# Queries, keys and probabilities turned by DRAM and block transposes, with a pair's steps set wider apart and a second GLU block ahead of the first pair

## The chip, the cores and the metric

The kernel runs on one core of a Trainium2 chip. The time is that of the whole execution in microseconds (us), as the device measures it. Before the change three runs took 1937.97, 1940.64 and 1940.51 us; their median is 1940.51 us. A core has five engines that work side by side, each with its own queue of instructions in a fixed order: PE (matrix multiplication), DVE (elementwise work and block transposes), ACT (activation functions and copies), POOL (here it issues DMAs) and SP (it issues the loads of the weights). An instruction that waits for something holds up everything behind it on its engine.

## The reference

Two layers over 256 positions and 2048 channels, in float32. Each layer normalises its input, multiplies by one wide input matrix, and splits the product into two branches:

```python
h = rmsnorm(x, norm_g)
proj = h @ w_in        # c_a, c_glu, c_gate, q_down, kv_down, k_pe, m_gate, g_conv, g_mla
y_conv = conv_branch(...) @ w_proj_conv   # GLU, causal depthwise conv of width 31, layernorm, silu, gate
y_mla = mla_branch(...) @ w_proj_mla      # q = rmsnorm(q_down) @ w_uq, k and v = rmsnorm(kv_down) @ w_ukv,
                                          # per-head norm, rope, block-causal softmax over 16 heads, gate
y = sigmoid(g_conv) * y_conv + sigmoid(g_mla) * y_mla
return x + y @ w_out
```

A head has 128 channels without position, 64 with rope (the rope key is shared by all heads) and 128 value channels. Positions are in chunks of 64; a query sees the keys of its own and of earlier chunks.

## The kernel before

**Products.** Every product has the activations as stationary operand and streams the weights, in blocks of up to 512 columns. To keep float32 accuracy each weight and each activation is split into a high and a low part, and `product` adds three matmuls: high by high, high by low and low by high (L222 to L224). Weights come in pieces of four 128-row tiles by SP's queue (`load`, L167) into three buffers; `split` makes the high part on ACT (L179) and the low part on DVE (L180) for two tiles at a time, up to two splits ahead of the matmuls, with three buffers of each part. One split feeds twelve matmuls; this is the unit of time of the program, and I call it a slot. A 512-column matmul follows the one before it by 0.227 us, so a slot is 2.73 us.

**Order of the blocks of a layer.** Three blocks of the down projection, GLU block 0, then for each of eight pairs of heads: the queries of the pair (`uq`, 2 slots), its keys and values (`ukv`, 2 slots) and, but for the last, the next GLU block (8 slots). After the pairs come four blocks each of `mgate`, `gmla`, `pmla`, `cgate`, `gconv`, `pconv` and `wout`.

**Work beside the products.** After each slot `background` takes one step from the queue `attn` (the attention of the pairs) and as many from `fill` (the taps of the convolution, two DVE instructions each at L657, and later the layernorm and the gate of branch A) as a budget allows: 0.65 units a slot while pairs run, 0.7 units a tap; from `mgate` on the rest of the fill is spread over the `20 * 8 - 4` slots before `pconv`. A planner then writes each engine's order: it goes by the program's order as priority and by its own estimate of when an instruction's data is there, and it puts the splits 100 instructions sooner (`SPLIT_SOONER`).

**A pair's steps.** `uq_evac` and `ukv_evac` copy the products out of PSUM and sum squares on ACT. Then `attention` appends eight steps, one for each of the next slots: `stats` (the two norms, key scaling and rope, on DVE), `turn_rope` twice, `turn_nope` twice, `scores`, `turn_p`, `values`. The three turning steps transpose 128x128 tiles on PE into PSUM (L537, L524, L599 to L603): 4 for rope, 8 for nope, 6 for the probabilities, and ACT and DVE split what stands in PSUM into high and low parts.

**The other way of turning**, already in use for the GLU and the gates: `park` writes a 128-row tile to DRAM with four DMAs of 32 rows each, so that the 32x32 blocks change places; `fetch` reads it back with one DMA; a DVE instruction transposes each 32x32 block (L257). All these DMAs are issued by POOL (L238, L246), and the fetch waits there until the parks have landed. `turn` puts the DVE step six splits later.

The functions around the change, with the line numbers of the profile:

Of the kernel before, what the change touches and what calls it, by code (L numbers as in the profile page):

```python
# [59 lines left out]
TURNED_AFTER = 6  # L60
SUMS_AFTER = 1
# [19 lines left out]

def blocks_of_layer():

    s = {"win": [], "wuq": [], "wukv": [], "wpc": [], "wpm": [], "wo": []}
    for _, n in DOWN_BLOCKS:
        s["win"].append(n)
    s["win"] += [512] * 24
    s["wuq"] = [2 * QK] * NPAIR
    s["wukv"] = [2 * (NOPE + VH)] * NPAIR
    for w in ("wpc", "wpm", "wo"):  # L90
        s[w] = [512] * 4
    return s
# [3 lines left out]
def trunk(ctx: ExitStack, tc: tile.TileContext, xT, x, g_in, pos, win, wuq, wukv, wpc, wpm, wo, cst, rows, invf, out):  # L96
# [43 lines left out]
    for l in range(DEPTH):  # L140
        order = [("down", i, "win") for i in range(len(DOWN_BLOCKS))] + [("glu", 0, "win")]
        for b in range(NPAIR):
            order += [("uq", b, "wuq"), ("ukv", b, "wukv")]
            if b + 1 < 8:
                order.append(("glu", b + 1, "win"))
        for kind, s in (
            ("mgate", "win"), ("gmla", "win"), ("pmla", "wpm"),
            ("cgate", "win"), ("gconv", "win"), ("pconv", "wpc"), ("wout", "wo"),
        ):
            order += [(kind, i, s) for i in range(4)]  # L150
        plans.append([(k, i, plan(l, s)) for k, i, s in order])

    loaded, done = {}, {}
# [16 lines left out]
    def split(i):  # L170
# [10 lines left out]
        done[i] = hi, lo  # L181
        while deferred and deferred[0][0] <= i:
            with tc.issue_after(ins.ins):
                deferred.popleft()[1]()
# [5 lines left out]
    budget = {"fill": 0.0, "rate": 0.0, "slots": 0}  # L190

    def background():
# [51 lines left out]
    def fetch(d, n):  # L244
        z = wide_p.tile([P, 4, n // P, 32], F32, tag="w", name="turned")
        nc.gpsimd.dma_start(z.rearrange("p i c s -> p (i c s)"), d.rearrange("j s i e -> (j s) (i e)"))  # L246
        return z

    def turn(src, n, use, dst=None):
# [3 lines left out]
        z = fetch(park(src, n, turn_d), n)  # L253
# [119 lines left out]
    for l in range(DEPTH):  # L373
# [85 lines left out]
        def pair_of(b, pairs=pairs, v_split=v_split):  # L459
            if b not in pairs:  # L460
                pairs[b] = dict(
                    q=work2.tile([P, T, 2, QK], F32, tag="q", name="q"),
                    k=work2.tile([P, T, 2, NOPE], F32, tag="k", name="k"),
                    r=work2.tile([P, 2, T, 2, ROPE], F32, tag="r", name="r"),
# [6 lines left out]
        def uq_evac(b, t, ps, pair_of=pair_of):  # L471
            p = pair_of(b)
            nc.scalar.copy(p["q"][:, t].rearrange("p h d -> p (h d)"), ps)
            for h in range(2):
                junk = work.tile([P, 512], F32, tag="junk", name="junk")
                nc.scalar.activation(
                    junk[:, :QK], ps[:, h * QK : (h + 1) * QK], AF.Square, accum_out=p["ss"][:, 0, t, h : h + 1]
                )

        def ukv_evac(b, t, ps, pair_of=pair_of):  # L480
            p = pair_of(b)
            v = ps.rearrange("p (h a d) -> p h a d", h=2, a=2)
            nc.scalar.copy(p["vh"][:, t], v[:, :, 1, :])
            nc.vector.tensor_sub(p["vl"][:, t], v[:, :, 1, :], p["vh"][:, t].bitcast(F32))
            nc.scalar.copy(p["k"][:, t], v[:, :, 0, :])
            for h in range(2):
                junk = work.tile([P, 512], F32, tag="junk", name="junk")
                nc.scalar.activation(junk[:, :NOPE], v[:, h, 0, :], AF.Square, accum_out=p["ss"][:, 1, t, h : h + 1])

        def attention(b, pair_of=pair_of, ss_d=ss_d, kpe=kpe, ccq=ccq, ssq_t=ssq_t, gqk=gqk, nope_t=nope_t, rope_t=rope_t, rope_k=rope_k, rope_l=rope_l, o_sb=o_sb, pt_h=pt_h, pt_l=pt_l, rinv=rinv):  # L490
# [3 lines left out]
            def stats():  # L494
                ss, q, k = p["ss"], p["q"], p["k"]
# [7 lines left out]
                rk = r[:, 1].unsqueeze(3)  # L503
                nc.vector.tensor_mul(k, k, rk.broadcast_to([P, T, 2, NOPE]))
                nc.vector.tensor_mul(
                    p["r"][:, 1], kpe.unsqueeze(2).broadcast_to([P, T, 2, ROPE]), rk.broadcast_to([P, T, 2, ROPE])
                )
                qr = q[:, :, :, NOPE:]
                qa = work.tile([P, T, 2, ROPE], F32, tag="qa", name="qa")
                qb = work.tile([P, T, 2, ROPE], F32, tag="qb", name="qb")  # L510
                nc.vector.tensor_mul(qa, qr, ccq.unsqueeze(2).broadcast_to([P, T, 2, ROPE]))
                nc.vector.tensor_mul(qb, qr, ssq_t.unsqueeze(2).broadcast_to([P, T, 2, ROPE]))
                qr = p["r"][:, 0]
                nc.vector.tensor_sub(qr[:, :, :, :HALF], qa[:, :, :, :HALF], qb[:, :, :, HALF:])
                nc.vector.tensor_add(qr[:, :, :, HALF:], qb[:, :, :, :HALF], qa[:, :, :, HALF:])
# [3 lines left out]
            def turn_nope(which):  # L519
                src = p["qk"[which]]  # L520
                tp = tp_p.tile([P, 2, SEQ], F32, tag="tp", name="tp_qk")
                for h in range(2):
                    for t in range(T):
                        nc.tensor.transpose(tp[:, h, t * P : (t + 1) * P], src[:, t, h, :NOPE], ident)  # L524
                hi, lo = nope_t[:, 2 * which], nope_t[:, 2 * which + 1]
                if which == 0:
                    nc.scalar.activation(hi, tp, AF.Copy, scale=gqk)
                    nc.vector.scalar_tensor_tensor(lo, tp, gqk, hi.bitcast(F32), op0=ALU.mult, op1=ALU.subtract)
                else:
                    nc.scalar.copy(hi, tp)  # L530
                    nc.vector.tensor_sub(lo, tp, hi.bitcast(F32))

            def turn_rope(which):
                src = p["r"][:, which]
                tp = tp_p.tile([P, SEQ], F32, tag="tp", name="tp_rope")
                for t in range(T):
                    nc.tensor.transpose(tp[:, t * P : (t + 1) * P], src[:, t].rearrange("p h d -> p (h d)"), ident)  # L537
                for h in range(2):
                    own, other = halves[h], halves[1 - h]
                    nc.scalar.copy(rope_t[own, which, h, :], tp[own])  # L540
                    if which == 0:
                        nc.vector.tensor_sub(rope_t[other, 0, h, :], tp[own], rope_t[own, 0, h, :].bitcast(F32))
                    else:
                        nc.scalar.copy(rope_t[other, 1, h, :], tp[own])
                        nc.vector.tensor_sub(rope_l[own, h, :], tp[own], rope_t[own, 1, h, :].bitcast(F32))

            def scores():
# [30 lines left out]
                pr = work.tile([P, 2 * P + 2 * SEQ], F32, tag="pr", name="pr")  # L578
                sums = small.tile([P, T, 2], F32, tag="sums", name="sums")
                at = 0  # L580
                st["pr"] = []
                for t, s, nkeys in ((0, s0, P), (1, s1, SEQ)):
                    for h in range(2):
                        dst = pr[:, at : at + nkeys]
                        nc.scalar.activation(
                            dst, s[:, h, :], AF.Exp,
# [3 lines left out]
                        st["pr"].append(dst)  # L590
                        at += nkeys
# [394 lines left out]
```

## Time and profile before

| | |
|---|---|
| median of the runs | 1940.51 us |
| the profiled execution | 1937.65 us, span 1935.8 us |
| PE busy | 1923.1 us, 99% of the span |
| DVE busy | 1582.1 us, 82% |
| ACT busy | 1101.3 us, 57% |
| POOL busy | 233.1 us, 12% |
| moved by DMA | 399.82 MB, 207 GB/s on the mean |
| granted TensorE clock | 1.0 throughout |

The span is the time from the first to the last instruction; the execution has 1.85 us around it. A row of a group of instructions reads: line, engine, operation, written tile <- read tiles, shape, count | busy time in us, mean length of one in ns | idle time of the engine just before them, and what ended most of it. Instructions of one engine overlap at their ends, so a group's busy time can be less than count times length. A row of waits reads: who <- for whom: us in total, times, longest.

By the order of the evacuations, the first layer has its GLU blocks and pairs from about 80 to 350 us, `mgate`, `gmla` and `pmla` to about 618, `cgate` and `gconv` to about 797, then `pconv` and `wout`; the second layer repeats this some 960 us later.

### The profile page before, as it was taken

What the parts mean: (1) busy time and instruction counts of PE and PEld (TensorE: products, weight loads), DVE (VectorE), ACT (ScalarE), POOL (GpSimd) and SP (SyncE); (2) the same over time, 40 slices, a digit from 0 to 9 for tenths busy, and PEclk for the clock granted to TensorE, in tenths of its full rate; (3) what the DMA queues carried; (4) which work ended last, traced back from release to release, by engine and by line L of the source; (5) the groups of instructions that cost most, each with busy time, mean ns of one, the idle gap of its engine ahead of it and who ended that gap; (6) DMA issues with size and microseconds to landing.
All of it is one profiled execution on the core that took longest, in us unless ns stands there. A gap on an engine that the chain in (4) does not pass through costs nothing.

```text
span 1935.8 us, 25532 instructions
## 1 busy us (share of the span) xinstructions
PE 1923.1 (99%) x9069; PEld 1623.8 (84%) x9069; DVE 1582.1 (82%) x2820; ACT 1101.3 (57%) x1750; POOL 233.1 (12%) x444
## 2 busy tenths in 40 slices
PE   9999999999999999999999999999999999999999
PEld 8888888888888887888898888888888888878887
DVE  7789998999999987466657899889999999864654
ACT  6667767664444457444556676776654435564443
POOL 0111111121000120021301121121210002101200
PEclk9999999999999999999999999999999999999999
DMA  7655555566555665566865554555665556655674
GB/s 290 220 178 182 185 177 183 192 212 228 191 191 193 216 243 190 201 240 231 272 237 196 180 190 176 179 187 200 218 218 196 196 191 212 239 191 206 241 254 142
DMA packets 72592, 399.82 MB, mean 207 GB/s; under 512 B 13056, under 2 KB 13072, under 8 KB 33552
## 3 DMA queue, kind: packets, MB, share of 16 engines
q1 hardware_dynamic: 55728, 361.44, 52.6%
q0 software_dynamic: 16736, 36.74, 6.0%
q8 instruction: 71, 1.16, 0.2%
q14 instruction: 57, 0.47, 0.1%
HBM read 376.64 MB, written 21.50 MB: 206 GB/s over the span
## 4 chain that ended last, share of the span: by engine, by line
PE 96%; DVE 1%; ACT 1%; issue 1%; DMA 0%; SPq 0%; DVEq 0%; ACTq 0%
PE acc L223 31%; PE acc L222 31%; PE acc L224 31%; PE o_ps L615 1%; PE s L569 1%; PE tp_qk L524 1%; ACT hi L179 1%; DVE v_t L700 0%; PE tp_rope L537 0%; DMA raw<-in_win 0%; ACT ycT L808 0%; DVE turned L798 0%; DVE v_t L802 0%; PE s L555 0%; DVE lo L180 0%
## 5 line engine op out<-in xcount | busy, mean ns | idle before, releaser
L179 ACT CAST hi<-raw 128x1024 fp32r<-128x1024 f32 (+2 forms) x688 | 703.5, 1024 | 716.8 <-PE acc L224 536.3
L180 DVE TENSOR_TENSOR lo<-raw,hi 128x1024 fp32r<-128x1024 f32 (+2 forms) x688 | 816.9, 1189 | 264.2 <-ACT hi L179 261.9
L657 DVE SCALAR_TENSOR_TENSOR v_t<-u_t,cst,v_t 128x256 f32<-128x256 f32 x960 | 414.9, 481 | 1.1
L223 PE MATMUL acc<-lo,h_hi 128*128 128x512 f32 (+2 forms) x864 | 334.3, 387 | 1.4 <-DVE lo L180 1.4
L223 PE MATMUL acc<-lo,hT 128*128 128x512 f32 (+2 forms) x864 | 333.3, 386 | 1.4 <-DVE lo L180 1.3
L224 PE MATMUL acc<-hi,h_lo 128*128 128x512 f32 (+2 forms) x864 | 331.7, 384 | 0.0
L224 PE MATMUL acc<-hi,hT 128*128 128x512 f32 (+2 forms) x864 | 331.0, 383 | 0.0
L222 PE MATMUL acc<-hi,h_hi 128*128 128x512 f32 (+2 forms) x864 | 302.5, 385 | 3.5 <-ACT hi L179 3.5
L222 PE MATMUL acc<-hi,hT 128*128 128x512 f32 (+2 forms) x864 | 301.8, 384 | 0.7 <-ACT hi L179 0.7
L238 POOL DMA_DIRECT2D turn_d<-gate x176 | 95.5, 550 | 803.7 <-ACT gate L792 459.4
L222 PEld LDWEIGHTS acc<-hi,h_hi 128*128 128x128 f32 x864 | 162.0, 189 | 34.0 <-ACT hi L179 4.7
L223 PEld LDWEIGHTS acc<-lo,h_hi 128*128 128x128 f32 x864 | 163.0, 189 | 32.5 <-DVE lo L180 3.8
L223 PEld LDWEIGHTS acc<-lo,hT 128*128 128x128 f32 x864 | 162.3, 188 | 32.0 <-DVE lo L180 3.3
L224 PEld LDWEIGHTS acc<-hi,h_lo 128*128 128x128 f32 x864 | 163.0, 189 | 28.9
L222 PEld LDWEIGHTS acc<-hi,hT 128*128 128x128 f32 x864 | 161.4, 188 | 30.6 <-ACT hi L179 1.1
L224 PEld LDWEIGHTS acc<-hi,hT 128*128 128x128 f32 x864 | 162.3, 188 | 28.8
L238 POOL DMA_DIRECT2D turn_d<-su x128 | 69.6, 550 | 484.2 <-DVE su L637 474.1
L223 PE MATMUL acc<-lo,yT 128*128 128x512 f32 x256 | 100.0, 390 | 0.0
L224 PE MATMUL acc<-hi,yT 128*128 128x512 f32 x256 | 99.6, 389 | 0.0
L223 PE MATMUL acc<-lo,ycT 128*128 128x512 f32 x256 | 99.6, 389 | 0.0
L224 PE MATMUL acc<-hi,oT 128*128 128x512 f32 x256 | 99.6, 389 | 0.0
L224 PE MATMUL acc<-hi,ycT 128*128 128x512 f32 x256 | 99.6, 389 | 0.0
(206 smaller groups left out, 2494.0 us busy)
## 6 DMA issues: line engine op xcount, KB each, us to landing
raw<-in_win SPq DMA_DIRECT2D x192, 1024.0 KB, 4.8
raw<-in_wpm SPq DMA_DIRECT2D x32, 1024.0 KB, 4.7
raw<-in_wpc SPq DMA_DIRECT2D x32, 1024.0 KB, 4.8
raw<-in_wo SPq DMA_DIRECT2D x32, 1024.0 KB, 4.9
raw<-in_wukv SPq DMA_DIRECT2D x16, 1024.0 KB, 4.7
turned<-turn_d POOLq DMA_DIRECT2D x50, 256.0 KB, 4.3
raw<-in_wuq SPq DMA_DIRECT2D x16, 768.0 KB, 4.3
raw<-in_win SPq DMA_DIRECT2D x15, 768.0 KB, 6.8
```

Of the source, the lines that this page charges most:

```text
L179: nc.scalar.copy(hi, r)
L180: ins = nc.vector.tensor_sub(lo, r, hi.bitcast(F32))
L222: nc.tensor.matmul(pts[t][:, :n], sh, hi[:, kk, :], start=first, stop=False)
L223: nc.tensor.matmul(pts[t][:, :n], sh, lo[:, kk, :], start=False, stop=False)
L224: nc.tensor.matmul(pts[t][:, :n], sl, hi[:, kk, :], start=False, stop=last)
L238: nc.gpsimd.dma_start(d[:, :, i, :].rearrange("j s e -> s j e"), src[32 * i : 32 * i + 32, :].rearrange("s (j e) -> s j e", j=4),)
L524: nc.tensor.transpose(tp[:, h, t * P : (t + 1) * P], src[:, t, h, :NOPE], ident)
L569: nc.tensor.matmul(s1[:, h, :], qa, ka, start=n == 0, stop=n == len(terms) - 1)
L615: nc.tensor.matmul(o_ps[:, h, kt * P :], v[j][:, kt, h, :], pt[i][:, h, queries], start=n == 0, stop=n == len(todo) - 1,)
L657: nc.vector.scalar_tensor_tensor(dst, src, w, dst, op0=ALU.mult, op1=ALU.add)
```

## The change

Queries, keys and probabilities are no longer transposed on PE. The columns of `w_uq` and `w_ukv` are put in another order ahead of the run, so that a pair's scaled keys, queries and both rope parts stand in one tile `qk` of 768 columns for each half of the positions, cut into 32-column blocks. `stats` writes them there and then parks and fetches each half in place; nine slots later `blockwise` transposes the blocks on DVE in place, and `split_rope` and `split_nope` make high and low parts from SBUF. The query gain is now applied in place on ACT ahead of the split. `scores` writes the probabilities of a pair into one tile of 768 columns and parks and fetches it; six slots later `split_p` transposes its blocks and splits it in two instructions.

The steps have slots of their own (`at_slot`): statistics in the first slot after the pair's keys, 60 instructions sooner in the planner's order; blocks and rope at 9, nope at 10 and 11, scores at 14, probabilities at 20, values at 22. Before, the eight steps took slots 1 to 8. The block transposes are put behind the newest low split on DVE (`issue_after`).

GLU blocks 0 and 1 both come ahead of the first pair, block `b + 2` follows pair `b`, and `cgate` block 0 stands between pairs 6 and 7. The fill's rate beside GLU blocks falls from 0.65 to 0.55 units a slot, and the slots over which the rest is spread from `20 * 8 - 4` to `19 * 8 - 4`. The layernorm's work tiles move to the new tile's buffers.

```diff
+QK_AFTER = 9
+P_AFTER = 6
...
+def order_of_layer():
+
+    order = [("down", i, "win") for i in range(len(DOWN_BLOCKS))] + [("glu", 0, "win"), ("glu", 1, "win")]
+    for b in range(NPAIR):
+        order += [("uq", b, "wuq"), ("ukv", b, "wukv")]
+        if b + 2 < 8:
+            order.append(("glu", b + 2, "win"))
+        elif b + 1 < NPAIR:
+            order.append(("cgate", 0, "win"))
...
+    def at_slot(ahead, f):
+        steps.append((clock[0] + ahead, f))
+
     def background():
+        clock[0] += 1
         if attn:
             attn.popleft()()
+        due = [f for slot, f in steps if slot <= clock[0]]
+        steps[:] = [e for e in steps if e[0] > clock[0]]
+        for f in due:
+            f()
...
-    def fetch(d, n):
+    def fetch(d, z):
+        nc.gpsimd.dma_start(z, d.rearrange("j s i e -> (j s) (i e)"))
...
+                qk=work2.tile([P, T, 4, 6, 32], F32, tag="qk", name="qk"),
+                qr=work2.tile([P, T, 2, 2, HALF], F32, tag="qr", name="qr"),
...
+            nc.scalar.copy(p["qk"][:, t, :, 0:2, :], ps[:, : 2 * NOPE].rearrange("p (j h c) -> p j h c", j=4, h=2))
+            nc.scalar.copy(p["qr"][:, t].rearrange("p a h c -> p (a h c)"), ps[:, 2 * NOPE :])
...
+                for t in range(T):
+                    rk = r[:, 1, t, :]
+                    k = qk[:, t, :, 2:4, :]
+                    nc.vector.tensor_mul(k, k, rk.unsqueeze(1).unsqueeze(3).broadcast_to([P, 4, 2, 32]))
...
+                for t in range(T):
+                    rows = qk[:, t].rearrange("p j i c -> p (j i c)")
+                    fetch(park(rows, 768, turn_d), rows)
...
-            def turn_nope(which):
...
+            def blockwise():
+                for t in range(T):
+                    z = p["qk"][:, t].rearrange("p j i c -> p (j i c)")
+                    with tc.issue_after(newest[0]):
+                        nc.vector.transpose(z, z)
+
+            def split_nope(which):
+                z = back[:, :, 2 * which : 2 * which + 2, :].rearrange("p b h s -> p h b s")
+                hi, lo = (nope_t[:, 2 * which + i].rearrange("p h (b s) -> p h b s", s=32) for i in range(2))
                 if which == 0:
+                    nc.scalar.activation(z, z, AF.Copy, scale=gqk)
+                nc.scalar.copy(hi, z)
+                nc.vector.tensor_sub(lo, z, hi.bitcast(F32))
...
-            def turn_p():
...
+                st["pr"] = pr.rearrange("p j h x c -> p (j h x c)")
+                fetch(park(st["pr"], 768, turn_d), st["pr"])
+
+            def split_p():
+                z = st["pr"]
+                with tc.issue_after(newest[0]):
+                    nc.vector.transpose(z, z)
+                z = z.rearrange("p (b i s) -> p i b s", i=6, s=32)
+                hi, lo = (a.rearrange("p h (x b s) -> p (h x) b s", x=3, s=32) for a in (pt_h, pt_l))
+                nc.scalar.copy(hi, z)
+                nc.vector.tensor_sub(lo, z, hi.bitcast(F32))
...
-            attn.append(stats)
-            for turn in (turn_rope, turn_nope):
-                for which in range(2):
-                    attn.append(lambda turn=turn, which=which: turn(which))
-            attn.extend((scores, turn_p, values))
+            def stats_soon():
+                with tc.high_priority(offset=60):
+                    stats()
+
+            at_slot(0, stats_soon)
+            at_slot(QK_AFTER, lambda: (blockwise(), split_rope(0), split_rope(1)))
+            for which in range(2):
+                at_slot(QK_AFTER + 1 + which, lambda which=which: split_nope(which))
+            at_slot(QK_AFTER + 5, scores)
+            at_slot(QK_AFTER + 5 + P_AFTER, split_p)
+            at_slot(QK_AFTER + 7 + P_AFTER, values)
...
-                budget["rate"] = 0.65
+                budget["rate"] = 0.55
...
-                    budget["slots"] = 20 * 8 - 4
+                    budget["slots"] = 19 * 8 - 4
```

More of the change, by code (lines that the diff above doesn't have):

```diff
@@ L140, in trunk @@
     for l in range(DEPTH):
[L141 to L153, printed above, removed]
+        plans.append([(k, i, plan(l, s)) for k, i, s in order_of_layer()])
+    loaded, done, newest = {}, {}, [None]
     deferred = deque()
@@ L533, in turn_rope @@
[L533 to L537, printed above, removed]
+                for t in range(T):
+                    rk = r[:, 1, t, :]
+                    k = qk[:, t, :, 2:4, :]
+                    nc.vector.tensor_mul(k, k, rk.unsqueeze(1).unsqueeze(3).broadcast_to([P, 4, 2, 32]))
+                    nc.vector.tensor_mul(
+                        qk[:, t, :, 5, :].rearrange("p (h a) c -> p h a c", h=2),
+                        kpe[:, t].rearrange("p (a c) -> p a c", a=2).unsqueeze(1).broadcast_to([P, 2, 2, HALF]),
+                        rk.unsqueeze(2).unsqueeze(3).broadcast_to([P, 2, 2, HALF]),
+                    )
@@ L538, in turn_rope, with split_rope @@
+            def split_rope(which):
+                z = back[:, :, 4 + which, :]
+                rt, rl = (a.rearrange("p i h (b s) -> p i h b s", s=32) for a in (rope_t, rope_l.unsqueeze(1)))
                 for h in range(2):
                     own, other = halves[h], halves[1 - h]
[L540 removed]
+                    nc.scalar.copy(rt[own, which, h], z[own])
                     if which == 0:
[L542 removed]
+                        nc.vector.tensor_sub(rt[other, 0, h], z[own], rt[own, 0, h].bitcast(F32))
```

150 lines of the change are left out of this document (71 added, 79 removed).

## Prediction

> **What bounds the kernel now.** I read the page's busy shares and its chain of waits first, then the waits of PE, then the groups of instructions with shapes kept apart, a timeline of PE where probabilities are turned, and a table of stages.
>
> ```profile
> PE 1923.1 (99%) x9069; PEld 1623.8 (84%) x9069; DVE 1582.1 (82%) x2820; ACT 1101.3 (57%) x1750; POOL 233.1 (12%) x444
> PE 96%; DVE 1%; ACT 1%; issue 1%; DMA 0%; SPq 0%; DVEq 0%; ACTq 0%
> PE acc L222 <- ACT hi L179: 4.2, 3, 2.8
> PE acc L223 <- DVE lo L180: 2.7, 4, 0.8
> ```
>
> PE is 99% busy, the chain is 96% PE, and PE waits 6.9 us in all for split weights. So an instruction taken from PE's queue comes off the time, as long as no new wait appears there.
>
> ```profile
> 215.48 0.27 PE L601 MATMUL tp_p<-ident,pr 128*128 128x128 f32 x1
> 215.59 0.27 PE L603 MATMUL tp_p<-ident,pr 128*128 128x128 f32 x1
> 215.70 0.27 PE L601 MATMUL tp_p<-ident,pr 128*128 128x128 f32 x1
> 215.80 0.27 PE L603 MATMUL tp_p<-ident,pr 128*128 128x128 f32 x1
> 215.83 0.48 PE L223 MATMUL acc<-lo,h_hi 128*128 128x512 f32 x1
> 216.15 0.39 PE L224 MATMUL acc<-hi,h_lo 128*128 128x512 f32 x1
> ```
>
> This timeline (start, length) gives the price of a transpose. Its length is 0.27 us, but the next one starts 0.11 us later; four of them and one 512-column matmul (pace 0.227 us elsewhere) take 216.15 - 215.48 = 0.67 us, so one costs (0.67 - 0.227)/4 = 0.11 us.
>
> ```profile
> 160.00:320.00 160.00, 160.00 (x817) 137.28 (x816) 146.40 (x327) 116.51 (x252) 24.86 (x47) 1.00 0.52 179
> 480.00:600.00 120.00, 120.00 (x531) 99.42 (x530) 116.27 (x206) 53.21 (x56) 0.00 (x0) 1.00 0.54 193
> 690.00:760.00 70.00, 67.91 (x294) 54.45 (x293) 61.58 (x93) 48.16 (x65) 8.61 (x16) 1.00 0.61 216
> 760.00:800.00 40.00, 40.00 (x178) 33.15 (x177) 17.58 (x16) 18.31 (x19) 0.00 (x0) 1.00 0.56 202
> ```
>
> Columns: stretch, length, busy PE, PEld, DVE, ACT, POOL, clock, DMA share, GB/s. In the pairs (160 to 320) DVE is at 91.5%; under the taps (480 to 600) it reaches 96.9% with PE still full, the highest load here that costs PE nothing; by 760 to 800 it is at 44%. DVE is the next limit.
>
> **The change, part by part.**
>
> *Transposes leave PE.* A pair has 4 rope, 8 nope and 6 probability transposes: 18, times 16 pairs is 288. At 0.11 us that is 31.7 us, all on the path. Nothing is added to PE.
>
> *DVE work per pair,* by the means of these rows:
>
> ```profile
> L180 DVE TENSOR_TENSOR lo<-raw,hi 128x768 fp32r<-128x768 f32 x64 | 61.1, 956 | 21.5 <-ACT hi L179 21.4
> L257 DVE STREAM_TRANSPOSE turned<-turned 128x512 f32<-128x512 f32 x34 | 24.0, 706 | 3.3 <-DMA turned<-turn_d 3.3
> L257 DVE STREAM_TRANSPOSE u_t<-turned 128x256 f32<-128x256 f32 x32 | 14.1, 440 | 5.5 <-DMA turned<-turn_d 5.5
> L504 DVE TENSOR_TENSOR k<-k,r_p 128x512 f32<-128x512 f32 x16 | 10.9, 684 | 0.0
> ```
>
> Three block transposes of 128x768: from 440 ns (256) and 706 (512) I extend to 0.97 us each, +2.91. The key multiply of 512 (0.684) becomes two of 256 (0.418 each, L511): +0.15. The shared-key multiply of 256 (0.415) becomes two of 128 (0.285, L514): +0.16. The low part of the queries loses its scale (0.746 to 0.685): -0.06. The low parts of probabilities, 0.686 + 0.417, become one of 768 (0.956): -0.15. Sum +3.0 us a pair, 24 us a layer, 48 us in all. Reading 32-element runs costs nothing extra: L750 does so and takes 685 ns, like the plain 512s.
>
> What covers it: DVE is idle 720 - 638 = 82 us between 80 and 800 of the first layer (the seven-stage table of that stretch). PE's time there falls by 8 x 2.0 = 16 us, which leaves 82 - 24 - 16 = 42 us, 94% load; below the 96.9% that cost PE nothing. Within the pairs it is tighter: a period is 36.3 us now (the first query evacuations of pairs 1 and 6 start at 118.84 and 300.25: 181.4/5), and DVE does 91.5%, 33.2, of it. After: 33.2 + 3.0, less 1.4 because the tap rate falls from 0.65 to 0.55 (12 slots x 0.1/0.7 = 1.7 taps, two instructions each at a pace of 0.4), is 34.8 in 34.3. So about 0.5 to 1.5 us of taps a period must slip past the last pair. They can: splits are ordered ahead of taps, and the taps' deadline is the last cgate/gconv stretch with the 44% above. If this cover is gone, PE pays the excess itself (first rival).
>
> *ACT per pair:* the query evacuation of 384 (0.481) becomes 256 (0.370) and 128 (0.28), twice: +0.34; the in-place scale (0.688) is now followed by a copy (0.614, L749): +0.61; probabilities in one copy: -0.12. +0.83 us a pair on an engine 73% busy in this stage (116.51 of 160): to 80%, no cost; ACT's longest queue is the hi copies, which wait for PE. The gate block moved between pairs 6 and 7 may add a table load or two of 1.28 us, covered likewise.
>
> *POOL and its queue:* 15 more DMAs a pair at 0.55 us, 8.3 us in a period of 34.3 on an engine 16% busy: to 40%. Between parks and the fetch POOL stands 1.9 to 5.0 us; now the two parks of queries and keys, the park of probabilities and the two GLU parks share the queue, and the GLU block's fetch can be queued behind a fetch that has not its data. In the gate blocks eight parks go out side by side (4.33 us), so the two query parks need not stand behind the first fetch.
>
> *DMA:* 3 x 0.393 MB out and back is 2.4 MB a pair, 69 GB/s on top of 179; the first 40 us of the kernel move 318 GB/s. No cost; the raw weight loads, landing in 4.8 us, may land some tenths later, ahead of their use by two pieces.
>
> *Latency of a turn, a new wait.* A GLU turn in the trace: first park at 198.54, fetch at 205.28, DVE reads at 209.00: 10.5 us; four parks 2.2, gap 3.5, issue 0.56, landing 3.7. For 768 columns in pairs of turns: 4.4 + 3.5 + 1.1 + about 5 (256 KB lands in 4.3) = 14 us. Ahead of it the statistics (204.92 to 213.9: 9 us). 23 us, against QK_AFTER = 9 slots, that is 8 x 2.73 after the step, plus 2 of scores: 23. Probabilities: scores to last exponential 9.5 us (203.9 to 213.4) and a turn of 12: 21, against 6 slots: 16. So a transpose can come up in DVE's queue as much as 5 us ahead of its data. It is pinned only behind the newest low split, so while DVE stands there the next low split stands too; PE holds up to two splits (5.5 us). Bounds: 0, as the GLU turns cost DVE 5.5 us and PE nothing, to 3 us a pair (5 us less a lead of 2; PE's weight loads stood for a low split 11 times, 1.2 us at most, so its lead is not always the full 5.5). I take 0.15 us a pair, 2 us in all, as the nearest row is the GLU turn itself, built and queued alike; and the written order is no deadline, for o_ps already comes 47 us after the pair's key evacuation (95.9 to 143.3), where eight slots would be 22: the planner puts a step where it expects its data.
>
> Tile for tile, the rows above make a 128x128 transpose 0.11 us on PE and 0.97/6 = 0.16 on DVE, with five DMAs for six of them; only PE's share lies on the path now. The Trainium skill, "VectorE: DVE Perf Modes", Rules for kernel authors, says to transpose 128x128 on TensorE where a PSUM destination will do, which speaks against this change. By that rule, the sum would be 288 x 0.05 = 14 us slower instead of 31.7 faster, were DVE's share on the path as PE's is. The trace agrees with it on the two prices; that DVE's share reaches the path is the first and second rival.
>
> *Second GLU block ahead, gate block later:* the same blocks of PE work in another order; zero. It gives taps work before the first pair. The number of slots after the pairs falls from 156 to 148, 22 us less in which the fill runs; with 42 us of DVE idle left I cost it at zero.
>
> *Sum:* -31.7 + 2 = -29.7. Against the profiled execution, 1937.65 (span 1935.8 and 1.85 around it): 1908. The median shown is 1940.51, 2.9 above; against it 1910.8. I give 1911.
>
> **The rivals.**
> 1. *DVE becomes the bound in the pairs and its taps do not slip.* For: 34.8 us of work in 34.3. At the best load seen, 96.9%, the period is 35.9 instead of 34.3: 1.6 us lost in about 14 periods, 23 us: 1934. Against: the planner already lets pair steps lag by 25 us and more.
> 2. *Late turns stop the low splits (the other side).* DVE stands in front of a transpose whose fetch has not landed, the next low split stands behind it, and PE after the 2 us lead. 3 us a pair is 48 us: 1940.5 - 31.7 + 48 = 1957. It decides from 2.0 us a pair. For: the 5 us computed for probabilities, POOL's five turns in a period, DVE with no idle time to catch up. Against: the GLU turns cost PE nothing.
> 3. *The two nearly cancel:* some periods of each, within 0.2%.
> That the transposes stay on PE is excluded by the diff.
>
> **How the numbers follow.** Forecast 0.54 (its own range 1904 to 1919), first rival 0.12 (of it 0.02 no change), second 0.30, the third 0.02, others 0.02, half of them faster. Faster 0.54 + 0.10 + 0.01 = 0.65; same 0.02 + 0.02 = 0.04; slower 0.30 + 0.01 = 0.31. A change under 0.2% (4 us) can't be told from none here. The range goes from 1903 (the full 31.7 off the lowest run shown, 1938, and most of the 2.1 us a layer that PE stands between 690 and 760, 67.91 of 70, should the new order of the fill remove it) to 1958, the second rival's price; its worse half lies outside.
>
> **What would show it.** Right: no L524/L537/L599-603 group, PE's matmul count lower by 288, PE still 99%, DVE near 85% overall, three 768-wide block transposes a pair at 0.97 us, DVE idle before them under 1 us each, PE waits for low splits under 10 us. First rival: DVE over 97% and PE under 97% between 160 and 340. Second: large idle before the block transposes released by DMA, PE waiting on L180's successor, or key/value evacuations held because the values step of two pairs before is late. Wrong also if the fill ends late and PE stands at the first pconv block.

## The result: slower, 2069.78 us

The changed kernel takes 2069.78 us in the median (2067.96 to 2070.27), against 1940.58 for the kernel before on the same chip: a ratio of 1.0666, 95% interval 1.0648 to 1.0685. The prediction was 1911 us, with 1958 as its upper end; it is wrong by sign and by size, 129 us the other way. The profiled execution has a span of 2068.0 us and a mean granted clock of 0.971.

The page of the kernel after: the row of busy times, and the row of the chain of waits.

```profile
PE 1950.6 (94%) x8781; PEld 1626.1 (79%) x8781; DVE 1624.3 (79%) x2884; ACT 1126.4 (54%) x1786; POOL 365.4 (18%) x684
...
PE 70%; DVE 14%; ACT 7%; DMA 5%; issue 3%; POOL 2%; ACTq 0%; SPq 0%; DVEq 0%; POOLq 0%
```

The 288 transposes are gone (9069 - 8781), but PE stands: 94% busy instead of 99%, and the chain is 70% PE instead of 96%. DVE, the engine I feared, is at 79%, less than before. Where the chain now runs is told by the table of stages of the kernel after, in its first layer (stretch, length, busy PE, PEld, DVE, ACT, POOL, granted clock, DMA share, GB/s):

```profile
200.00:240.00 40.00, 34.88 (x152) 29.20 (x151) 27.00 (x64) 23.78 (x52) 11.99 (x22) 0.87 0.52 165
240.00:280.00 40.00, 29.15 (x122) 24.41 (x121) 30.40 (x71) 22.28 (x55) 8.09 (x16) 0.83 0.44 151
...
400.00:440.00 40.00, 30.91 (x124) 25.44 (x125) 26.86 (x64) 21.00 (x50) 8.19 (x15) 0.75 0.41 138
...
480.00:720.00 240.00, 238.14 (x1066) 196.46 (x1065) 225.43 (x381) 118.75 (x137) 25.22 (x46) 1.00 0.60 214
```

From 480 to 800 us PE is full (from there to 960 us the gaps hold 5 us). Nearly all is lost in the pairs, and there no engine is near its limit: in 240 to 280, PE 73%, DVE 76%, ACT 56%, and the DMA engines 44%, where they had 55% in the same stretch before. So it is latency, a chain of waits, that sets the pace. Taking the starts of consecutive matmuls, gaps of over 0.7 us hold 120 us of standing (beyond a matmul's pace of 0.227) after the change, 8 us before it.

The waits of the kernel after (engine, line waited for: us in total, times, longest):

```profile
POOL turn_d L252 <- DVE qk L534: 153.7, 14, 24.8
...
PEld acc L236 <- ACT junk L512: 35.3, 8, 6.3
...
PEld acc L237 <- DVE lo L184: 25.2, 29, 2.2
...
ACT pv L507 <- PE o_ps L644: 9.0, 4, 4.0
...
ACT qk L492 <- DVE qk_t L568: 4.8, 4, 1.6
```

PE's longest wait is for L512, the last squares of a key/value evacuation: PE has a next product, but no free PSUM buffer, since the one before is not evacuated. And L507, the first instruction of that evacuation, which writes the high part of the values, waits for L644, the value matmuls, of *another* pair. The timeline of the kernel after shows such a place (start, length, instruction, idle before and its releaser):

```profile
311.97 1.30 PE L644 MATMUL o_ps<-pv 128*128 128x128 f32 x10
...
312.91 0.65 ACT L507 CAST pv<-acc 128x256 fp32r<-128x256 f32 x2 [1.21 <-PE o_ps L644]
```

`v_split` has two sets of V tiles, and pair b takes set `b % 2`. So the V evacuation of pair b can't start before the value matmuls of pair b-2 have read their set. From the rows of these two lines I took, for each pair, the start of the V evacuation and the start of the last value matmul, some 0.3 us ahead of its end (us, first layer):

| | pair 0 | 1 | 2 | 3 | 4 | 5 |
|---|---|---|---|---|---|---|
| before: V evacuation starts | 91.0 | 122.8 | 159.6 | 197.6 | 233.8 | 270.4 |
| before: last value matmul | 144.6 | 183.7 | 222.9 | 262.2 | 301.8 | 340.4 |
| after: V evacuation starts | 112.8 | 144.2 | 208.4 | 267.2 | 312.9 | 357.3 |
| after: last value matmul | 208.3 | 264.7 | 313.0 | 357.5 | 411.9 | 453.4 |

Read it across: after, the V evacuation of pair 2 starts at 208.4, with the last value matmul of pair 0 at 208.3; pair 3 at 267.2 behind 264.7, pair 4 at 312.9 with 313.0, pair 5 at 357.3 with 357.5. Before, it had 15.0, 13.9, 10.9 and 8.2 us in hand at the same pairs. From V evacuation to the end of the values a pair took 54 to 70 us then; now it takes 90 to 120, while two periods of 36.3 us are all that two sets allow.

Before, the twelve value matmuls of pair 2 were done 11 us ahead of the V evacuation of pair 4 at 233.8:

```profile
221.62 1.53 PE L615 MATMUL o_ps<-pv 128*128 128x256 f32 x12
```

Why 120 in pair 1? GpSimd's timeline in the kernel after:

```profile
231.79 4.36 POOL L252 DMA_DIRECT2D turn_d<-qk  x8 [4.07 <-DVE qk L534]
236.14 1.10 POOL L252 DMA_DIRECT2D turn_d<-pr  x2
237.76 0.55 POOL L252 DMA_DIRECT2D turn_d<-pr  x1 [0.53 <-DMA turn_d<-qk]
239.51 0.55 POOL L252 DMA_DIRECT2D turn_d<-pr  x1 [1.20 <-DMA turn_d<-qk]
240.06 0.56 POOL L259 DMA_DIRECT2D qk<-turn_d  x1
241.25 0.56 POOL L259 DMA_DIRECT2D qk<-turn_d  x1 [0.63 <-DMA turn_d<-pr]
245.96 0.54 POOL L259 DMA_DIRECT2D pr<-turn_d  x1 [4.16 <-DMA turn_d<-pr]
```

The exponentials of pair 1 ended at 215.7, but their parks go out only at 236.1: in GpSimd's order they stand behind the eight parks of the queries and keys of pair 2, and these wait for the statistics of pair 2, which need the squares that stand behind its V evacuation on ACT, and that waited for the values of pair 0. So there is a ring: values of b-2, V evacuation of b, statistics of b, query parks of b, probability parks of b-1 (by the queue's order alone), block transpose, values of b-1, V evacuation of b+1. A turn of it takes 44 to 59 us (the steps of the row of V evacuations from pair 2 to pair 5), and a pair period, 36.3 us before, can't be shorter.

V is not the only tile that is short. `qk` has two buffers as well, and the query evacuation of pair 4 (L492) starts as soon as the last split of pair 2 (L568) has read its buffer:

```profile
256.78 1.29 DVE L568 TENSOR_TENSOR qk_t<-qk,qk_t 128x512 fp32r<-128x512 f32 x2 [0.25 <-ACT qk_t L567]
...
258.27 0.36 ACT L492 COPY qk<-acc 128x256 f32<-128x256 f32 x1
```

Pairs 6 and 7 stand likewise, at 356.86 and 404.20 behind 356.77 and 404.17.

Last, the price that I had feared, in the groups of the kernel after (busy, mean ns | idle before):

```profile
L560 DVE STREAM_TRANSPOSE qk<-qk 128x768 f32<-128x768 f32 x32 | 30.4, 965 | 1.7 <-DMA qk<-turn_d 1.7
...
L631 DVE STREAM_TRANSPOSE pr<-pr 128x768 f32<-128x768 f32 x16 | 15.6, 974 | 0.6 <-DMA pr<-turn_d 0.4
```

The three block transposes a pair take 0.97 us each, as predicted, and DVE stood before them 2.3 us in the whole run.

### The profile page after: what moved, and what is told of

It is laid out like the page before. It is cut to its first block, busy times and chain, and to the rows that moved or that the text cites. A ratio compares the mean times of both kernels' runs of the same rounds, so it can differ in the third digit from the quotient of the medians.

```text
span 2068.0 us, 25491 instructions
## 1 busy us (share of the span) xinstructions
PE 1950.6 (94%) x8781; PEld 1626.1 (79%) x8781; DVE 1624.3 (79%) x2884; ACT 1126.4 (54%) x1786; POOL 365.4 (18%) x684
## 4 chain that ended last, share of the span: by engine, by line
PE 70%; DVE 14%; ACT 7%; DMA 5%; issue 3%; POOL 2%; ACTq 0%; SPq 0%; DVEq 0%; POOLq 0%
PE acc L237 23%; PE acc L238 23%; PE acc L236 23%; DVE lo L184 4%; DVE v_t L692 4%; POOL turn_d L252 1%; ACT pr L618 1%; ACT hi L183 1%; DMA turn_d<-pr 1%; DMA turn_d<-xres 1%; ACT L618 1%; DMA pr<-turn_d 1%; DMA xres<-in_x 1%; ACT qk_t L575 1%; DVE qk L560 1%
## 5 line engine op out<-in xcount | busy, mean ns | idle before, releaser
L236 PE MATMUL acc<-hi,qkc 128*128 128x384 f32 (+1 forms) x256 | 100.0, 406 | 46.0 <-ACT junk L512 21.7
L237 PE MATMUL acc<-lo,qkc 128*128 128x384 f32 (+1 forms) x256 | 100.3, 392 | 0.1
L252 POOL DMA_DIRECT2D turn_d<-qk x128 | 69.8, 553 | 172.9 <-DVE qk L534 153.7
L238 PE MATMUL acc<-hi,qkc 128*128 128x384 f32 (+1 forms) x256 | 100.0, 391 | 0.0
```

The costliest lines, as they stand in the source:

```text
L236: nc.tensor.matmul(pts[t][:, :n], sh, hi[:, kk, :], start=first, stop=False)
L237: nc.tensor.matmul(pts[t][:, :n], sh, lo[:, kk, :], start=False, stop=False)
L238: nc.tensor.matmul(pts[t][:, :n], sl, hi[:, kk, :], start=False, stop=last)
L252: nc.gpsimd.dma_start(d[:, :, i, :].rearrange("j s e -> s j e"), src[32 * i : 32 * i + 32, :].rearrange("s (j e) -> s j e", j=4),)
```

## The experiments

The first theory is the ring: V tiles reused too soon, and the probabilities behind the queries on GpSimd's queue. Its rivals are the new order and spacing by themselves, DVE's added work, and DVE or PE standing for late turns. Line numbers shift by a few between kernels.

**New order of the blocks alone** (the kernel before, with `order_of_layer`, the rate 0.55 and 19 slots; all transposes on PE, steps in slots 1 to 8).

> The kernel before with only the new order of the blocks (two GLU blocks ahead of the first pair, the first gate block of branch A between pairs 6 and 7), the fill's rate of 0.55 and 19 blocks of slots; transposes stay on PE and a pair's steps keep slots 1 to 8. If the reused V buffers, POOL's queue or the wide spacing make the loss (theories 1 to 3), this stays within 5 us of 1940. If the new order or rate makes it (theory 4), it is at 2000 or more.

Measured 1939.4 us, ratio 0.9988 (0.9976 to 0.9999). The second GLU block, the moved gate block and the slower taps cost nothing, as predicted.

**The same with the wide spacing** (statistics with priority at slot 0, rope at 9, nope at 10 and 11, scores at 14, probabilities at 20, values at 22; still on PE).

```diff
-            attn.append(stats)
...
-            attn.extend((scores, turn_p, values))
+            at_slot(0, stats_soon)
+            at_slot(QK_AFTER, lambda: (turn_rope(0), turn_rope(1)))
...
+            at_slot(QK_AFTER + 7 + P_AFTER, values)
```

> The same new order, and a pair's steps in the wide slots (rope at 9, scores at 14, probabilities at 20, values at 22), but every transpose still on PE and no DMA added. Theory 1 (a pair's chain is longer than the two pair periods after which its V buffers are written again, and DRAM latency is part of that length) and theory 2 (POOL's queue): 1940 to 1960, since 22 slots are 60 us against two periods of 73. Theory 3 (the spacing alone is too wide, with any way of turning): 2000 or more, with PE waiting for accumulators held by key/value evacuations.

Measured 1949.43 us, 1.0047 (1.0035 to 1.0059). The spacing costs 10 us with no turn by DRAM at all. Its rows show why: V evacuations at 183.3, 221.0, 257.8, 298.7 and 338.3, the last value matmuls of two pairs before at 183.4, 221.1, 257.9, 298.7 and 338.4. A chain of 71 to 81 us already uses up two periods.

**A third set of V tiles in the changed kernel.** The tiles `pv` and `qk_t` have room at their ends, so nothing else moves.

```diff
-        qk_t = big.tile([P, 14 * SEQ], F32R, tag="big", name=f"qk_t{l}")
+        qk_t = big.tile([P, 16 * SEQ], F32R, tag="big", name=f"qk_t{l}")
-        pv = big.tile([P, 3584], F32R, tag="big", name=f"pv{l}")
+        pv = big.tile([P, 4096], F32R, tag="big", name=f"pv{l}")
+        v_split.append([a.rearrange("p (t h d) -> p t h d", t=T, h=2) for a in (pv[:, 3584:], qk_t[:, 14 * SEQ :])])
...
-                    vh=v_split[b % 2][0],
-                    vl=v_split[b % 2][1],
+                    vh=v_split[b % 3][0],
+                    vl=v_split[b % 3][1],
```

> The changed kernel with a third set of V buffers, in parts of two tiles that were unused, so that a pair's V is overwritten three pairs later and not two. Theory 1: most of the 129 us come back, 1915 to 1960. Theory 2 (probabilities' parks stand on POOL behind the next pair's query parks, whatever frees V): above 2020. Theory 4: unchanged near 2070.

Measured 1961.09 us, 1.0105 (1.0057 to 1.0152): 109 of the 129 us are back by a place to put V, with every turn, DMA and DVE instruction of the change still there. It is 1 us above the range, but the reuse of V two pairs later is shown to be the main cause. The row of busy times on its page:

```profile
PE 1904.7 (97%) x8781; PEld 1599.1 (82%) x8781; DVE 1614.8 (82%) x2884; ACT 1126.0 (57%) x1790; POOL 364.2 (19%) x684
```

and of its waits:

```profile
PEld s L605 <- ACT qk_t L580: 19.6, 2, 10.1
...
PEld acc L237 <- DVE lo L184: 17.4, 23, 1.8
```

What is left has its own signs: once in each layer PE stands 10 us for the rope splits of one pair. The V evacuations of pairs 4 and 5 still start 1.1 and 2.1 us behind the values of pairs 1 and 2, so three sets are barely enough for a chain of 95 to 127 us. And `qk` still holds: the query evacuations of pairs 4, 6 and 7 start at 257.12, 330.09 and 367.85, 0.0 to 0.2 us behind its last reading by the pair two before.

**Probabilities back on PE in the changed kernel**, turned one slot after the scores, values at slot 16; queries and keys by DRAM, two V sets.

> The changed kernel with the probabilities turned on PE again, one slot after the scores, values one slot later (16 in place of 22); queries and keys still go by DRAM. 96 transposes return to PE, 10.6 us. Theories 1 and 2 both: the chain loses six slots and POOL's queue the parks in dispute, so the time falls to between 1919 (1940.5 - 31.7 + 10.6) and 1950. Theory 4: above 2040.

Measured 1970.36 us, 1.0152 (1.0103 to 1.0202). A shorter chain (73 to 95 us) is worth nearly as much as a third set. It is a miss all the same, 20 us above the range: the V evacuations still start within 0.2 us of the last value matmul, so V holds this kernel too.

**Only the order on GpSimd's queue.** The four parks of the probabilities are issued by ACT, their fetch by SP.

```diff
-                fetch(park(st["pr"], 768, turn_d), st["pr"])
+                fetch(park(st["pr"], 768, turn_d, nc.scalar), st["pr"], nc.sync)
```

> The changed kernel, two V sets as it has them, with the probabilities' four parks issued by ACT and their fetch by SP, so that they no longer stand in POOL's queue. Theory A (a loop: values of pair b-2, V evacuation of pair b, its statistics, its query parks, behind them on POOL the parks of the probabilities of pair b-1, values of pair b-1; 45 to 50 us a turn where a period has 34): the loop is cut at POOL, so most of the loss goes, 1935 to 1980, as with a third V set (1961). Theory B (the chain of one pair is simply longer than two periods, POOL's order has no part): 2030 or more, as the chain keeps its length.

Measured 2013.79 us, 1.0378 (1.0336 to 1.0421): 56 us back, so the parks on GpSimd's queue are the second part of the ring. The time lies between the ranges of the two theories, since V still holds the pairs (evacuations at 204.0, 239.6, 291.6; values of two pairs before at 204.1, 239.7, 291.9). The Trainium skill, "DMA: Bandwidth & Descriptors", SWDGE vs HWDGE vs iDMA, would have plain transfers issued from SP or ACT, not GpSimd. The run agrees, with its 56 us; it doesn't part the other path of issue from the order in which the parks stood. The traces show that the order had a large share: in the kernel after, the probability parks of pairs 1 to 6 go out 13 to 21 us behind the last exponential, here 0 to 14 us.

**Narrower slots in the changed kernel** (`QK_AFTER` 6, `P_AFTER` 3).

> The changed kernel with QK_AFTER 6 and P_AFTER 3 in place of 9 and 6: scores at slot 11, probabilities at 14, values at 16. In the planned order POOL now parks the probabilities of pair b-1 ahead of the queries of pair b. Theory A: the loop is cut by the order alone, 1935 to 1985. Theory B: the shorter written chain gives back part, 16 of 60 us a pair at most where latency allows: 1990 to 2040. If latency alone sets the chain and no order matters: 2060 or more.

Measured 2020.13 us, 1.0411 (1.0356 to 1.0466): 50 us back by two constants, in the range of theory B: the shorter chain gives back a part, and the order alone doesn't cut the ring. The V evacuations still follow the values (205.2 with 205.3, 293.0 with 293.1).

**Both, third V set and probabilities off GpSimd's queue.**

> Three V sets and the probabilities off POOL's queue. Theory A: below the 1961 of three V sets alone, as the 10 us stall of PE at 243 us and at 1219 us (two pairs' query parks, probabilities and a GLU park side by side on POOL, the fetch late) goes too: 1930 to 1955. If what was left in that kernel is DVE's load and the late fill: 1955 to 1965.

Measured 1966.23 us, 1.0133 (1.0092 to 1.0174): with V free the queue's order is worth nothing more, against the expectation that the two would add; it lies 1 us above both ranges. In this kernel's waits another evacuation is named:

```profile
PEld acc L236 <- ACT hi L183: 16.2, 14, 3.5
...
PEld acc L236 <- ACT junk L498: 12.4, 6, 3.3
```

L498 is the squares of the queries: the next tile with two buffers is `qk`, which holds queries and keys until they are split.

**A third `qk` tile, and its control.** To make room the pool `wide` goes from 6 buffers to 4 and `sx` shares a buffer in both; only the second has the third tile.

```diff
-    wide_p = pool("wide", 6)
+    qk_p = pool("qk3", 3)
+    wide_p = pool("wide", 4)
...
-                    qk=work2.tile([P, T, 4, 6, 32], F32, tag="qk", name="qk"),
+                    qk=qk_p.tile([P, T, 4, 6, 32], F32, tag="qk", name="qk"),
```

> Control for the run with a third query/key tile: three V sets, probabilities parked by ACT and fetched by SP, and to make room 4 in place of 6 of the 512-column work tiles and the scores' small tile in the buffer of a statistics tile. Expected near the 1966 of the same kernel with 6 work tiles, up to 15 us more if the work tiles bind.

> The control with a third query/key tile of 768 columns a half. If, once V is out of the way, the query evacuations wait for the tile of the pair two before (19 us of PE's weight loads stood behind evacuation squares in the kernel with three V sets): 10 to 25 us below the control. If the rest of the loss is DVE's load in the pairs and the late fill: within 5 us of the control.

The control took 1977.68 us (1.0184, 1.0152 to 1.0217), the third tile 1955.62 (1.0073, 1.0051 to 1.0094): 22 us by the `qk` tile. Some 11 of them may only undo what the smaller pool lost (1977.68 against 1966.23, two runs each, whose intervals overlap). A buffer is again what held: with two buffers the query evacuation of pair 4 started at 257.13, 0.1 us behind the last reading of pair 2 (257.08), with three at 253.34, 4 us ahead of it (257.32).

**With V (and `qk`) free, probabilities on PE.**

> The kernel with queries and keys by DRAM and probabilities on TensorE (1970.4 us), with a third set of V tiles. Theory A (buffer reuse: a pair's values come too late for the V evacuation of the pair after next): the third set frees the evacuations, the time falls to 1945-1958 us, below the 1961.1 us of three V sets with probabilities by DRAM, because the pair's chain is also shorter. Theory B (with probabilities on TensorE the chain is short enough for two V sets, and the rest of the loss is the query/key tile or the late turns themselves): no more than 4 us come back, 1966-1971 us.

> Three V sets, three query/key tiles (1955.6 us with probabilities by DRAM), probabilities back on TensorE. Theory A (two short buffers and the probability path are all that is lost): 1925-1940 us, as the query/key transposes that are gone are worth some 20 us. Theory B (late query/key turns cost by themselves: splits of weights behind the block transposes on VectorE): 1945-1955 us.

Three V sets and probabilities on PE: 1952.31 us, 1.0065 (1.005 to 1.008), 18 us less than with two sets; V no longer holds (evacuations at 216.4 and 250.8, values of three pairs before at 189.9 and 233.4). With the third `qk` tile, and the smaller pool it needs, 1956.95 (1.009, 1.0072 to 1.0107), a miss: I expected 1925 to 1940. So with three V sets and two `qk` tiles 192 transposes have left PE, some 20 us at 0.106, and the kernel is still 13 us slower than before. By the starts of matmuls, this kernel's intervals of over 0.26 us hold 29 us more than before, about half of that in the pairs and the other half between 720 and 800 us of each layer, where the fill ends. The timeline there, in the kernel with three V sets and probabilities on PE:

```profile
757.14 1.28 ACT L745 ACT_TABLE_LOAD   x1
758.43 4.04 ACT L745 ACTIVATE v_t<-v_t,cst 128x256 f32<-128x256 f32 x8
...
762.38 1.03 ACT L183 CAST hi<-raw 128x1024 fp32r<-128x1024 f32 x1
```

Eight activations of the fill go in a row on ACT, and the high part of the next weights stands behind them; PE stands 4.5 us there. That this follows from fill pushed later by the pairs is argued from the trace; no run isolates it.

**Only the probabilities by DRAM.** First at the wide slots, with two and with three V sets:

> New order of blocks and wide slots, queries and keys on PE, only the probabilities by DRAM: 96 transposes leave PE, 10.6 us; the loop has no query parks in it. Against the 1949 of the same slots with all transposes on PE. Theory A: 1938 to 1960, no large loss. Theory B (the latency of the probabilities' turn makes the chain too long): 1980 or more.

> The kernel that turns only the probabilities by DRAM, at the wide slots (1941.9 us), with a third set of V tiles. Theory A: its pair chain fits into two pair periods, as no loss of matmul starts above that of the kernel before is left beyond 13 us, so a third set brings 0-4 us, 1938-1942 us. Theory B: a part of those 13 us is V tiles still held: 1930-1937 us, and faster than the kernel before.

1941.94 us (1.0001, 0.9989 to 1.0012) and 1938.55 (0.9992, 0.9982 to 1.0001). Against the same slots with everything on PE (1949.43) the 96 transposes of the probabilities are worth 7.5 us of the 10.2 that 0.106 us each would give. The 3.4 us of the third set are not clear of the noise, as the intervals of the two ratios overlap. So the step that the change makes can pay for itself where nothing waits for it; it only pays for the spacing it needs.

Then at narrow slots, values at 14, in the new order and in the old:

> New order of blocks with PE transposes for queries and keys and the narrow slots of the kernel before (rope 2 and 3, nope 4 and 5, scores 6), and only the probabilities by DRAM, split at slot 12, values at 14. 96 transposes leave PE: 1939.4 (new order alone) less 10.6. If a turn by DRAM costs nothing where no loop and no long chain stand behind it: 1929 to 1933. If a turn costs PE something of its own (DVE's 1 us more a pair, the late block transposes): 1936 to 1942.

> The same on the kernel before itself: its own order of blocks, rate 0.65, only the probabilities by DRAM, split at slot 12, values at 14. If the new order has no part in the gain or loss: the same as the run with the new order within 4 us, 1929 to 1936; if the second GLU block ahead is needed for DVE's load, 1938 or more.

1972.34 us (1.0163, 1.0135 to 1.019) and 1967.09 (1.0132, 1.011 to 1.0155): 30 us or more above the gain I hoped for. The two lie close, so the new order of the blocks has little part in it. Three runs looked for the reason: the statistics with priority, as at the wide slots; a third V set; and that with the probabilities off GpSimd's queue.

> The kernel that turns only the probabilities by DRAM at narrow slots (1972.3 us), with the stats step issued ahead of its place as in the change. In that kernel pair 0's exponentials were parked 16 us later than in the same kernel at wide slots, which has this priority (181 against 165 us). Theory C (the stats step without priority falls behind weight splits and fill, and the chain is late from there): 1935-1950 us. Theory D (the narrow slots themselves, or GLU turns ahead on GpSimd's queue, make the probabilities late): 1965-1975 us.

> The kernel that turns only the probabilities by DRAM at narrow slots (1972.3 us), with a third set of V tiles. In that kernel the V evacuation of pairs 3, 4, 5 and 6 starts 0.1-0.4 us after the last value matmul of pairs 1, 2, 3 and 4 (225.2 after 224.8, 271.3 after 271.2, 314.1 after 313.9, 363.1 after 363.0). Theory A (the same reuse of V; ScalarE waits in order, so the next pair's exponentials stand behind it): the third set brings most of the 33 us back, 1935-1948 us, and the V evacuations no longer start with the values' end. Theory D (GpSimd's queue, or the narrow slots): 1965-1972 us.

> The same kernel with the probabilities' parks issued by ScalarE and their fetch by SyncE. Theory A: with V free the order on GpSimd's queue holds nothing, the time is that of the kernel with a third V set within 4 us. Theory D: if that one stays above 1960 us, this one comes to 1935-1950 us.

1973.67 us (1.0174, 1.0159 to 1.0189), so not the priority. 1970.33 (1.0144, 1.0118 to 1.0169): my theory of the V tiles falls here. The evacuations of pairs 4 and 5 do come free (253.8 and 284.7 instead of 271.3 and 314.0), but the values don't follow: from pair 0 to pair 4 they end 45 to 52 us apart (225.7, 272.9 and 317.8 for pairs 1 to 3, 363.2 for pair 4), a pair's chain grows from 61 us in pair 0 to 146 in pair 7, and pair 7 waits for V again (363.2). 1952.92 us (1.006, 1.0039 to 1.0081) with the parks on ACT: moving them off GpSimd's queue gives 17 of the 30 us, 3 us above the range. There the order has little part: with GpSimd the parks go out 0.3 us behind the exponentials, and of the eight fetches of the first layer only two stand in line, for 2 and 5 us. But from the last exponential to the block transpose a turn takes 10.8 to 16.1 us, with ACT and SP 7.3 to 12.2.

Why the narrow slots lose what the wide ones don't stays open. A slower turn it is not: at the wide slots with three V sets it takes 9.9 to 19.5 us. In both kernels the last scores of a pair come behind the values of the pair before, so that scores, exponentials, turn and values of one pair follow those of the other, slower than a period of 36 us. What differs in the traces of pairs 1 to 5 is that the last score matmul comes 15 to 20 us behind those values at the narrow slots and 11 to 14 at the wide ones, where the first score matmul already stands ahead of them (257.5 against 276.7). No run shows whether this makes the loss.

No version ran clearly below the kernel before; the nearest are the new order alone (0.9988) and probabilities by DRAM at wide slots with three V sets (0.9992).

## Why the prediction was wrong, point by point

- *Transposes leave PE, 31.7 us:* the count is right, and so is the price. Taking every group in the kernel before that is followed by two products, from its first start to the second product's start less 0.227, 250 transposes cost 26.6 us, 0.106 each. That makes 30.5 us for the 288. The gain is real but not seen, as PE stands 112 us more in long gaps.
- *DVE +3.0 us a pair, ACT +0.83:* right in size (0.97 us a block transpose) and harmless. The first rival, DVE as the bound, is wrong: 76% in 240 to 280.
- *POOL 16% to 40%:* the load was counted, the order was not. I asked whether the GLU's fetch stands behind another fetch, not whether the probability parks of one pair stand behind the query parks of the next. Taking them off that queue was worth 56 us, and with a third V set nothing.
- *Latency of a turn:* 14 us, and 12 for probabilities, were too short (pair 2's first park at 231.8, its block transposes from 249.5: 18 us; pair 1's probabilities 236.1 to 255.6: 19) and, more, they were put to the wrong question. I weighed them against the slots and asked whether DVE would stand in front of a late transpose. DVE waited 2.3 us. A park of 96 KB lands in 5.3 us by the page of after, on top of waits in line.
- *"The written order is no deadline":* this is the step that failed; by it the sum has only 2 us for all that comes late. It is true of the slots, and the planner did put the steps later. But there was a deadline: the V set of a pair must be read before the evacuation of the pair two further on, and so must its `qk` buffer. I even had the number, 47 us from key evacuation to `o_ps`, and took it as freedom; against two periods of 36.3 us it is a part of a budget of which the kernel before had 15 to 3 us left (pair 7: evacuation at 343.7, values of pair 5 until 340.4). Fourteen slots more between keys and values used up all of it: with every transpose on PE they cost 10 us, and with turns by DRAM on top the chain came to 90 to 120 us and the time to 129 us more.
- *Second rival, late turns stop the low splits, 48 us:* right sign, wrong place and far too small. The true mechanism stood only as a sign in the last part of the prediction (evacuations held because the values of two pairs before are late); it had no price.
- *Second GLU block and moved gate, zero:* right, by the run of the order alone.

## What to carry to other kernels

When work is made later, don't ask first which engine gets busier, but which buffer is held longer: list every tile that the moved step reads, its number of sets, and the time from its writing to its last reading, and compare that with sets times period. Here that sum, from two rows of the profile before, gave 3 to 15 us of slack against a delay of tens. And where several pairs' transfers share one in-order queue, write out who stands ahead of whom, for a later pair's early step can hold an earlier pair's late one and so close a ring.

## What the runs showed of the hardware

PE's standing costs more than its length. After a gap of 6.01 us the kernel after shows the products starting at another pace (timeline: start, length):

```profile
271.48 0.80 PE L236 MATMUL acc<-hi,qkc 128*128 128x512 f32 x1 [6.01 <-DVE lo L184]
272.07 0.63 PE L237 MATMUL acc<-lo,qkc 128*128 128x512 f32 x1
272.50 0.63 PE L238 MATMUL acc<-hi,qkc 128*128 128x512 f32 x1
...
276.69 0.40 PE L236 MATMUL acc<-hi,qkc 128*128 128x512 f32 x1
276.92 0.39 PE L237 MATMUL acc<-lo,qkc 128*128 128x512 f32 x1
277.15 0.39 PE L238 MATMUL acc<-hi,qkc 128*128 128x512 f32 x1
```

For 5 us a 512-column product starts every 0.43 us, then every 0.23; the granted clock is 0.50 from 269.8 to 276.5 us and 1.00 behind that. I sorted the steps of up to 0.7 us from one matmul to the next by the granted clock. Where it was 0.5, 119 weight products took 0.40 us each in the mean instead of 0.22, and 132 score and value products 0.24 instead of 0.12: 38 us lost to pace, on top of the 112 to standing. Less the 30.5 us of the transposes that makes 120 of the 132 us by which the span grew; the rest I can't place. The Trainium skill, "TensorE: Matmul & The Clock Gate", Why this matters for your kernels, says that a gap of more than about 3 us drops the clock to half; this trace agrees, with 0.43 against 0.227. It doesn't show 3 us as a bound, though: the clock was also 0.50 from 256.1 to 262.9 us, after gaps of 2.70 and 2.12 us with two matmuls between them. I had priced every wait at its length alone.

GpSimd also stood 0.53 and 1.20 us before probability parks until parks of the queries had landed, which these do not read. Why they wait there, no run tells.
